# Prompt attention: a unit's value products issued behind its last transpose, and exponentials over up to 1024 columns

## The chip, the core and the metric

The kernel runs on one core of a Trainium2 chip. The metric is the device time of one launch in microseconds, the median of the timed runs. Engines are named as in the profile: PE is TensorE's matmul and PEld its weight load, DVE is VectorE, ACT is ScalarE, POOL is GpSimd, SP the engine that issues most DMAs.

## What is computed

One inference step of a decoder layer: an input projection, two kinds of heads (forgetting attention and a matrix memory), an output projection with layer norm, and an MLP with a second layer norm, for 2048 prompt tokens and for 64 sample tokens that attend to a paged cache. The change touches the forgetting attention of the prompt alone: 8 heads of 64 columns, blocks of 128 queries.

```python
def block(args):
    q_i, L_i, i = args
    s = jnp.einsum('bqhd,bkhd->bhqk', q_i, k).astype(jnp.float32) * scale
    s = s + L_i[..., :, None] - L[:, :, None, :]
    q_pos = i * Q_BLOCK + jnp.arange(Q_BLOCK)
    s = jnp.where(k_pos[None, :] <= q_pos[:, None], s, -jnp.inf)
    p = jax.nn.softmax(s, axis=-1)
    return jnp.einsum('bhqk,bkhd->bqhd', p.astype(v.dtype), v)
```

L is the running sum of the logarithms of the forget gates. The term L_i is the same along a row and drops out of the softmax, so the kernel adds only the negative sum of the keys (tile `nl`).

## The kernel before

The kernel has stages: the projections (with the matrix memory beside them), prompt attention (`phase_b`), the output projection (`phase_o`) and the MLP (`phase_c`). The sample tokens' attention to the cache is spread over the others by a pacer (`tick`), which counts up microseconds and now and then lets the next step in. In `phase_b` its pace is infinite, so that `tick` lets nothing in there.

A tile framework places the instructions: it takes them in the order in which the Python code writes them, with dependencies found from the tiles, and a scheduler that models times sets each engine's order at build. Each engine then runs its queue in that order. A tile of a pool with `bufs=n` has n places; whoever takes one waits until an earlier holder's last reader is done. `tc.issue_after(x)` adds no wait, only an order: instructions in the block come behind x on x's engine.

`phase_b` does 64 units, 8 heads times 8 pairs of query blocks. Unit g of a head has the query blocks qt = 2g and 2g+1, and query block qt has n = 128 (qt + 1) keys.

- `scores` (one unit ahead of `values`): for each query block, and for each 512 keys, two matmuls into a PSUM bank `pS` (lines 970 and 971; queries are split into a high part `qh` and a rest `ql`), from three banks in turn. VectorE adds `nl`, writes the score tile `S` and keeps the maximum in `mx` (lines 977 and 981, the latter for the diagonal block, whose mask `nd` GpSimd makes on line 963). `S` is 128 x 512, ten places.
- `values`: ScalarE takes the exponential of each `S` tile in place, with the row's sum into `lp` (line 998), and VectorE adds the sums (line 999). TensorE transposes the weights in blocks of 128 x 128, up to four into one PSUM bank `pt` (line 1011, three banks); ScalarE or VectorE copies a bank to `PT` (lines 1014 and 1016; `PT` holds four key blocks by 256 queries, four places). Then the value products (line 1020): for key block k a matmul with `vn` as weights into `po`, even k in the upper half of the array's columns and odd k in the lower. In the code, the products of four key blocks stand behind those blocks' transposes; ahead of the next four. At the end ScalarE copies the upper half and VectorE adds the lower (lines 1026 and 1028), and every fourth unit `finish` divides by the sums and stores.

A value product reads four-byte operands and leaves two records in the trace; the built program holds it as one.

Of the kernel before, what the change touches and what calls it, by code (L numbers as in the profile page):

```python
# [52 lines left out]
def body(ctx, tc, I, O, stages):  # L53
# [836 lines left out]
    def phase_b():  # L890
# [61 lines left out]
        def scores(z, g):  # L952
# [4 lines left out]
            for i in range(2):  # L957
# [8 lines left out]
                for a in range(0, n, 512):  # L966
                    b = min(n, a + 512)
                    w = max(b - a, 256)
                    pS = bank()
                    T.matmul(pS[:, :w], qh[:, qs], ks[:, a:a + w], start=True, stop=False)  # L970
                    last["PE"] = T.matmul(pS[:, :w], ql[:, qs], ks[:, a:a + w], start=False, stop=True)
                    tick(0.42)
                    sp = pb.tile([128, 512], F32, name="S", bufs=10)
                    st.append(sp)
                    e = min(b, qt * 128)
                    if e > a:
                        last["DVE"] = V.tensor_tensor_reduce(out=sp[:, :e - a], in0=pS[:, :e - a], in1=nl[:, a:e], scale=1.0, scalar=NEG,
                                               op0=OP.add, op1=OP.max, accum_out=mx[:, j:j + 1])
                        j += 1
                    if b == n:  # L980
                        V.tensor_tensor_reduce(out=sp[:, e - a:b - a], in0=pS[:, e - a:b - a], in1=nd, scale=1.0, scalar=NEG,
                                               op0=OP.add, op1=OP.max, accum_out=mx[:, j:j + 1])
                        j += 1
# [4 lines left out]
        def values(z, g, sc):  # L988
# [3 lines left out]
            for i, (st, mx) in enumerate(sc):  # L992
                qt = 2 * g + i
                n = (qt + 1) * 128
                lp = pb.tile([128, 4], F32, name="lp", bufs=6)
                for k, sp in enumerate(st):
                    w = min(512, n - k * 512)
                    last["ACT"] = A.activation(sp[:, :w], sp[:, :w], AF.Exp, bias=mx[:, 7:8], accum_out=lp[:, k:k + 1])  # L998
                V.tensor_reduce(z["ls"][:, qt:qt + 1], lp[:, :len(st)], axis=AX.X, op=OP.add)

            po = ppb.tile([128, 256], F32, name="po", bufs=1)
            nk = 2 * g + 2
            for k0 in range(0, nk, 4):
                PT = pb.tile([128, 4, 256], F32, name="PT", bufs=4)
                for i in range(2):
                    kk = min(4, 2 * g + i + 1 - k0)
                    if kk <= 0:
                        continue
                    pt = ppb.tile([128, 4, 128], F32, name="pt", bufs=3)
                    for k in range(kk):  # L1010
                        T.transpose(pt[:, k], sc[i][0][k0 // 4][:, k * 128:(k + 1) * 128], ident)
                    dst = PT[:, :kk, i * 128:i * 128 + 128]
                    if i == 0 or (k0 // 4) % 2 != 0:
                        A.copy(dst, pt[:, :kk])
                    else:
                        V.tensor_copy(dst, pt[:, :kk])
                for k in range(k0, min(k0 + 4, nk)):
                    q0 = 128 if k == nk - 1 else 0
                    c = (k % 2) * 64
                    last["PE"] = T.matmul(po[c:c + 64, q0:], z["vn"][:, k], PT[:, k - k0, q0:],  # L1020
                                          start=(k < 2), stop=(k >= nk - 2), skip_group_check=True)
                tick(0.45 * min(4, nk - k0))
            if g % 4 == 0:
                z["ot"] = pb.tile([64, 1024], F32, name="ot", bufs=2)
            od = z["ot"][:, (g % 4) * 256:(g % 4) * 256 + 256]
# [912 lines left out]
```

## Time and profile before

| | us |
|---|---|
| median of 3 timed runs | 3253.03 (3247.86 to 3255.45) |
| profiled execution | 3243.8 |
| its span, first to last instruction | 3241.8 |
| prompt attention, first score matmul to last value product | 879.1 to 1318.7, 439.6 |
| of it: 640 records of score matmuls, 1088 transposes, 1152 records of value products | |

The profile is of one execution. A row of the timeline has the start, the length, the engine, the line, the tiles (out <- in), the shape, and a count where like instructions are merged; in brackets stands the idle time before it and who ended it. A row of a window has the stretch, its length, and for PE, PEld, DVE, ACT and POOL the busy time with the number of instructions, then the clock that was granted to TensorE (1.00 is full), the DMA engines' share and GB/s. Matmuls overlap, so that the distance from one start to the next, not the length, is what one costs TensorE.

### The profile page before, as it was taken

To read this page: it belongs to the slowest core of one execution; us is meant where nothing else is said; L and a number is where in the kernel's file an instruction comes from. 1 tells how busy PE (TensorE), PEld (TensorE's weight loads), DVE (VectorE), ACT (ScalarE), POOL (GpSimd) and SP (SyncE) were. 2 spreads that over 40 slices of the span, in tenths; PEclk is the share of its full clock that TensorE was granted. 3 is DMA by queue.
4 is the path that set the end of the run, shared out by engine and by line. 5 is a ranking of instruction groups with operands and counts; after the bars stand their busy time and mean duration, and the time that the engine had idled before them with its cause. 6 is when DMAs were issued, how large, how long until landed. Compare 5 with 4: busy or idle time off the path is not lost.

```text
span 3241.8 us, 58017 instructions
## 1 busy us (share of the span) xinstructions
PE 3132.6 (97%) x21681; PEld 2552.5 (79%) x21681; DVE 2105.9 (65%) x5083; ACT 1502.6 (46%) x2965; POOL 916.0 (28%) x974
## 2 busy tenths in 40 slices
PE   8999999999899999999999999999999999899997
PEld 8898999999866667677677777677777777788895
DVE  6856557465488887543556568565686666866658
ACT  4343344334388888412444445343453444544442
POOL 0121324333333333475333324333334121000000
PEclk9999999999999999999999999999999999999998
DMA  5565866777676865686787869778879566543332
GB/s 189 147 214 168 263 216 243 255 244 264 195 257 169 203 177 126 223 297 243 291 297 268 305 241 335 296 265 313 295 282 342 201 231 215 188 164 119 116 105 100
DMA packets 339777, 734.36 MB, mean 227 GB/s; under 512 B 63656, under 2 KB 177704, under 8 KB 338600
## 3 DMA queue, kind: packets, MB, share of 16 engines
q1 hardware_dynamic: 252360, 416.18, 39.7%
q0 software_dynamic: 83520, 304.12, 26.6%
q10 hardware_dynamic: 3616, 10.36, 0.9%
q8 instruction: 171, 2.80, 0.3%
q14 instruction: 110, 0.90, 0.1%
HBM read 677.71 MB, written 86.38 MB: 236 GB/s over the span
## 4 chain that ended last, share of the span: by engine, by line
PE 44%; DMA 4%; DVE 3%; issue 1%; POOL 0%; ACT 0%; DVEq 0%; ACTq 0%; POOLq 0%
PE ph L163 8%; PE ph L164 7%; PE ph L165 7%; PE py L163 6%; PE py L165 5%; PE py L164 5%; PE sO L1790 3%; DMA vt<-cache_v,idxV 2%; PE sQ L1678 2%; DMA xr<-cache_v,idxV 1%; DVE y L1351 1%; DVE wl L157 1%; PE sT L1747 1%; DMA kT<-cache_k,idxK 0%; POOL vt L1766 0%
## 5 line engine op out<-in xcount | busy, mean ns | idle before, releaser
L157 DVE TENSOR_TENSOR wl<-wr,wh 128x1024 fp32r<-128x1024 f32 x364 | 444.2, 1222 | 376.3 <-ACT wh L154 374.9
L154 ACT ACTIVATE wh<-wr 128x1024 fp32r<-128x1024 f32 x364 | 383.0, 1054 | 331.2 <-PE ph L164 175.7
L163 PE MATMUL ph<-x1h,wh 128*128 128x512 f32 (+1 forms) x1280 | 455.0, 355 | 1.1 <-ACT hq L1333 1.1
L164 PE MATMUL ph<-x1l,wh 128*128 128x512 f32 (+1 forms) x1280 | 452.5, 354 | 0.2 <-DVE x1l L157 0.2
L165 PE MATMUL ph<-x1h,wl 128*128 128x512 f32 (+1 forms) x1280 | 450.1, 353 | 0.0
L1655 POOL DMA_INDIRECT kT<-cache_k,idxK x256 | 275.6, 1077 | 536.3 <-PE sQ L1678 470.5
L163 PE MATMUL py<-wh,hh 128*128 128x512 f32 x896 | 357.3, 401 | 3.0 <-ACT hh L154 1.5
L164 PE MATMUL py<-wl,hh 128*128 128x512 f32 x896 | 352.5, 393 | 3.4 <-DVE wl L157 3.4
L165 PE MATMUL py<-wh,hl 128*128 128x512 f32 x896 | 350.0, 394 | 2.0 <-DVE hl L157 2.0
L1351 DVE TENSOR_TENSOR y<-y,py 128x512 f32<-128x512 f32 x416 | 280.6, 681 | 64.0 <-PE py L165 59.3
L163 PE MATMUL pm<-xh,whi 128*128 128x256 f32 (+1 forms) x1024 | 298.9, 292 | 0.0
L164 PE MATMUL pm<-xl,whi 128*128 128x256 f32 (+1 forms) x1024 | 294.8, 288 | 0.0
L165 PE MATMUL pm<-xh,wlo 128*128 128x256 f32 (+1 forms) x1024 | 293.8, 287 | 0.0
L1766 POOL DMA_INDIRECT vt<-cache_v,idxV x164 | 180.3, 1100 | 384.4 <-PE sO L1790 315.3
L163 PEld LDWEIGHTS ph<-x1h,wh 128*128 128x128 f32 x1280 | 240.4, 188 | 42.0 <-issue 7.8
L164 PEld LDWEIGHTS ph<-x1l,wh 128*128 128x128 f32 x1280 | 240.5, 188 | 33.8 <-issue 3.3
L165 PEld LDWEIGHTS ph<-x1h,wl 128*128 128x128 f32 x1280 | 240.1, 188 | 34.1 <-issue 3.7
L163 PE MATMUL pm<-whi,xh 128*128 128x256 f32 (+2 forms) x816 | 236.9, 291 | 9.2 <-ACT whi L154 8.2
L164 PE MATMUL pm<-wlo,xh 128*128 128x256 f32 (+2 forms) x816 | 232.5, 285 | 0.6 <-DVE wlo L157 0.6
L165 PE MATMUL pm<-whi,xl 128*128 128x256 f32 (+2 forms) x816 | 232.2, 285 | 0.0
L998 ACT ACTIVATE S<-S,mx 128x512 f32<-128x512 f32 (+2 forms) x320 | 207.8, 653 | 19.0 <-DVE mx L984 17.6
L163 PEld LDWEIGHTS py<-wh,hh 128*128 128x128 f32 x896 | 168.6, 189 | 51.4 <-issue 10.9
(372 smaller groups left out, 6799.7 us busy)
## 6 DMA issues: line engine op xcount, KB each, us to landing
wr<-w SPq DMA_DIRECT2D x224, 512.0 KB
wr<-dw SPq DMA_DIRECT2D x128, 512.0 KB
wra<-w_in SPq DMA_DIRECT2D x104, 512.0 KB
dw<-w POOLq DMA_DIRECT2D x48, 512.0 KB, 8.4
Rb<-dR SPq DMA_DIRECT2D x128, 128.0 KB
xn<-xp_t SPq DMA_DIRECT2D x16, 512.0 KB
qn<-dq SPq DMA_DIRECT2D x128, 64.0 KB
kn<-k_prompt SPq DMA_DIRECT2D x64, 128.0 KB
```

Source lines behind the costliest of these rows:

```text
L154: last["ACT"] = A.activation(dst, src, AF.Copy, scale=scale)
L157: r = (eng or V).tensor_tensor(dst, src, hi.bitcast(F32), op=OP.subtract)
L163: T.matmul(ps, wh, xh, start=first, stop=False, skip_group_check=shared)
L164: T.matmul(ps, wh, xl, start=False, stop=False, skip_group_check=shared)
L165: last["PE"] = T.matmul(ps, wl, xh, start=False, stop=stop, skip_group_check=shared)
L998: last["ACT"] = A.activation(sp[:, :w], sp[:, :w], AF.Exp, bias=mx[:, 7:8], accum_out=lp[:, k:k + 1])
L1351: V.tensor_tensor(y, y, ps, op=op)
L1655: G.indirect_dma_start(out=piece(n), out_offset=None, in_=ck, in_offset=IO(ap=idxK[:, b, j // 2, j % 2:j % 2 + 1], axis=0))
L1678: r = T.matmul(pq[h4 * 32:h4 * 32 + 32, hg].rearrange("p (k c) -> p k c", k=2), z["qb"][:, hd], kv, start=(db == 0), stop=(db == 1), skip_ ...
L1747: T.transpose(p[:, f], z["U"][u][:, hg, f].rearrange("p k t -> p (k t)"), ident)
L1766: vx["last"] = G.indirect_dma_start(out=vt.rearrange("p f c -> p (f c)"), out_offset=None, in_=cv, in_offset=IO(ap=idxV[:, b, (kt % 4) * 4 ...
L1790: after_ = T.matmul(po[r:r + 32], z["PT"][:, hg, 2 * f + g, pg].rearrange("p h q -> p (h q)"), vts[f][:, g, hg * 256:(hg + 1) * 256], star ...
```

## The change

Two things change in `phase_b`. A score tile now has 1024 columns (seven places for ten), VectorE fills it in two steps of 512 as before, and one exponential covers up to 1024 columns; `lp` keeps two sums in place of four. And `values` writes all transposes and copies of a unit first, keeps its list of `PT` tiles, and then all its value products, each ordered behind the unit's last transpose (`turned`). The `tick` in `values` goes. `PT` keeps its four places, which is what the longest unit (16 key blocks) uses.

```diff
-                    sp = pb.tile([128, 512], F32, name="S", bufs=10)
-                    st.append(sp)
+                    if a % 1024 == 0:
+                        st.append(pb.tile([128, 1024], F32, name="S", bufs=7))
+                    sp = st[-1][:, a % 1024:a % 1024 + 512]
...
-                lp = pb.tile([128, 4], F32, name="lp", bufs=6)
+                lp = pb.tile([128, 2], F32, name="lp", bufs=6)
                 for k, sp in enumerate(st):
-                    w = min(512, n - k * 512)
+                    w = min(1024, n - k * 1024)
                     last["ACT"] = A.activation(sp[:, :w], sp[:, :w], AF.Exp, bias=mx[:, 7:8], accum_out=lp[:, k:k + 1])
...
+            PTs = []
             for k0 in range(0, nk, 4):
                 PT = pb.tile([128, 4, 256], F32, name="PT", bufs=4)
+                PTs.append(PT)
...
                     for k in range(kk):
-                        T.transpose(pt[:, k], sc[i][0][k0 // 4][:, k * 128:(k + 1) * 128], ident)
+                        c = k0 % 8 * 128 + k * 128
+                        turned = T.transpose(pt[:, k], sc[i][0][k0 // 8][:, c:c + 128], ident)
...
-                for k in range(k0, min(k0 + 4, nk)):
-                    q0 = 128 if k == nk - 1 else 0
-                    c = (k % 2) * 64
-                    last["PE"] = T.matmul(po[c:c + 64, q0:], z["vn"][:, k], PT[:, k - k0, q0:],
+            for k in range(nk):
+                q0 = 128 if k == nk - 1 else 0
+                c = (k % 2) * 64
+                with tc.issue_after(turned.ins):
+                    last["PE"] = T.matmul(po[c:c + 64, q0:], z["vn"][:, k], PTs[k // 4][:, k % 4, q0:],
                                           start=(k < 2), stop=(k >= nk - 2), skip_group_check=True)
-                tick(0.45 * min(4, nk - k0))
```

The scheduler then sets another order. TensorE's queue, in the longest unit of the fifth head (16 key blocks), before; the unit's own products read `po_15285`, its last transposes fill `pt_15338` and `pt_15343`, and the transposes into `pt_15407` and `pt_15410` and the scores belong to later units:

```order
L1011 MATMUL pt_15327<-ident_74,S_15150 128x128 x4
L1020 MATMUL po_15285<-PT_15286,vn_13898 64x256 x4
L970 MATMUL pS_15485<-ks_14708,qh_15452 128x512
...
L1020 MATMUL po_15285<-PT_15303,vn_13898 64x256 x4
L1011 MATMUL pt_15338<-ident_74,S_15130 128x128 x3
...
L1011 MATMUL pt_15343<-ident_74,S_15155 128x128 x4
L1020 MATMUL po_15285<-PT_15320,vn_13898 64x256 x4
L1011 MATMUL pt_15407<-ident_74,S_15253 128x128
L970 MATMUL pS_15500<-ks_14708,qh_15452 128x512
...
L1011 MATMUL pt_15410<-ident_74,S_15262 128x128 x2
...
L1020 MATMUL po_15285<-PT_15337,vn_13898 64x256 x3
L1020 MATMUL po_15285<-PT_15337,vn_13898 64x128
```

Where rows are left out there are only score matmuls: two stand between the first runs of products, two ahead of `pt_15343`, four ahead of `pt_15410` and four ahead of the last run. The products come in four runs. The same unit in the changed program, where each left-out row is the second score matmul of a pair:

```order
L1015 MATMUL pt_15166<-ident_74,S_14976 128x128 x3
L1015 MATMUL pt_15171<-ident_74,S_14999 128x128 x4
L1025 MATMUL po_15125<-PT_15126,vn_13798 64x256 x4
L1025 MATMUL po_15125<-PT_15139,vn_13798 64x256 x4
L1025 MATMUL po_15125<-PT_15152,vn_13798 64x256 x4
L1015 MATMUL pt_15247<-ident_74,S_15097 128x128
L970 MATMUL pS_15328<-ks_14576,qh_15290 128x384
...
L1015 MATMUL pt_15250<-ident_74,S_15106 128x128 x2
L970 MATMUL pS_15337<-ks_14576,qh_15290 128x512
...
L1025 MATMUL po_15125<-PT_15165,vn_13798 64x256 x3
L1025 MATMUL po_15125<-PT_15165,vn_13798 64x128
```

Four runs of products have become two: twelve products stand together behind the last transposes, and the last four follow behind three transposes and four score matmuls.

ScalarE's queue near the end of the stage, before; the exponentials are those of the last two query blocks (n = 1920 and 2048), the copies those of the last two units:

```order
L998 ACTIVATE S,lp<-S,mx 128x512 x3
L998 ACTIVATE S,lp<-S,mx 128x384
L1014 COPY PT<-pt 128x4x128 x3
L1014 COPY PT<-pt 128x128
L1014 COPY PT<-pt 128x2x128
L998 ACTIVATE S,lp<-S,mx 128x512 x4
L1014 COPY PT<-pt 128x4x128
```

And in the changed program:

```order
L999 ACTIVATE S,lp<-S,mx 128x1024
L999 ACTIVATE S,lp<-S,mx 128x896
L1018 COPY PT<-pt 128x4x128
L1018 COPY PT<-pt 128x128
L999 ACTIVATE S,lp<-S,mx 128x1024 x2
L1018 COPY PT<-pt 128x2x128
L1018 COPY PT<-pt 128x4x128
```

Eight exponentials have become four over the same columns, and the last block's stand ahead of two copies that they stood behind. Ahead of this stage the engines' orders are the same; behind it, TensorE's, VectorE's, ScalarE's and SP's differ in a few places by neighbours that change places, and GpSimd's not at all.

## The prediction

> **What bounds the kernel now.** I read the engines' totals first, to see which engine the time is made of, and then cut the span into stretches (busy time of each engine, granted clock and DMA share), to see the attention stage by itself.
>
> ```profile
> PE 3132.6 (97%) x21681; PEld 2552.5 (79%) x21681; DVE 2105.9 (65%) x5083; ACT 1502.6 (46%) x2965; POOL 916.0 (28%) x974
> ...
> 879.10:904.00 24.90, 18.41 (x92) 12.64 (x93) 15.70 (x69) 15.03 (x45) 4.71 (x11) 0.73 0.75 206
> 904.00:1308.00 404.00, 395.46 (x2712) 274.76 (x2710) 327.60 (x1296) 341.49 (x961) 145.33 (x225) 1.00 0.68 180
> 1308.00:1318.70 10.70, 10.07 (x82) 6.51 (x78) 3.21 (x10) 6.59 (x17) 0.26 (x1) 1.00 0.08 25
> ```
>
> Over the whole span TensorE is the bound, and prompt attention is the 439.6 us from 879.1 to 1318.7. In its long middle, TensorE is busy for 395.46 of 404.00 us, so it idles for 8.5 us; ScalarE is at 85% (341.49) and VectorE at 81% (327.60). The change removes no TensorE work, so it can gain in two ways only: TensorE's idle time, and what a change from one kind of matmul to another costs. The next view, waits on TensorE in that middle stretch (total, times, longest), says who ends the idle time.
>
> ```profile
> PE pt L1011 <- ACT S L998: 1.4, 3, 0.5
> PE pt L1011 <- ACT PT L1014: 1.2, 1, 1.2
> PE pS L970 <- DVE mx L977: 1.2, 1, 1.2
> PE pS L970 <- DVE ls L999: 1.0, 1, 1.0
> PE pS L970 <- DVE mx L981: 0.8, 2, 0.6
> PE po L1020 <- DVE ot L1028: 0.7, 1, 0.7
> PE pS L970 <- DVE mx L984: 0.4, 2, 0.2
> PE pt L1011 <- DVE PT L1016: 0.4, 2, 0.2
> PE pt L1011 <- DVE lt L1038: 0.2, 1, 0.2
> PE po L1020 <- ACT PT L1014: 0.2, 1, 0.2
> ```
>
> These add up to 7.5 us: 2.8 behind ScalarE (exponentials and copies of the transposed tiles) and 4.7 behind VectorE. They are few and short; no single place repeats at a price that matters.
>
> **The change: TensorE's order.** What does a change of kind cost? The timeline of TensorE from 1296 us on holds every kind (start, length, line, tiles, count; each value product leaves two records, so x16 is eight products).
>
> ```profile
> 1296.13 0.49 PE L1011 MATMUL pt<-ident,S 128*128 128x128 f32 x3
> 1296.37 0.47 PE L970 MATMUL pS<-ks,qh 128*128 128x512 f32 x1
> 1296.69 0.39 PE L971 MATMUL pS<-ks,ql 128*128 128x512 f32 x1
> 1296.92 1.03 PE L1011 MATMUL pt<-ident,S 128*128 128x128 f32 x8
> 1297.71 0.48 PE L970 MATMUL pS<-ks,qh 128*128 128x512 f32 x1
> 1298.03 0.40 PE L971 MATMUL pS<-ks,ql 128*128 128x512 f32 x1
> 1298.35 1.95 PE L1020 MATMUL po<-PT,vn 128*64 128x256 f32 x16
> 1300.23 0.44 PE L970 MATMUL pS<-ks,qh 128*128 128x384 f32 x1
> 1300.51 0.34 PE L971 MATMUL pS<-ks,ql 128*128 128x384 f32 x1
> 1300.69 0.60 PE L1011 MATMUL pt<-ident,S 128*128 128x128 f32 x4
> 1301.22 1.08 PE L1020 MATMUL po<-PT,vn 128*64 128x256 f32 x8
> 1302.23 0.50 PE L970 MATMUL pS<-ks,qh 128*128 128x512 f32 x1
> 1302.56 0.39 PE L971 MATMUL pS<-ks,ql 128*128 128x512 f32 x1
> 1302.79 0.39 PE L970 MATMUL pS<-ks,qh 128*128 128x512 f32 x1
> ```
>
> Read the starts, not the lengths, since matmuls overlap. Eight products take 1298.35 to 1300.23, 1.88 us; four take 1301.22 to 1302.23, 1.01 us. So a product is 0.2175 us, and a run of them pays 1.01 - 4 x 0.2175 = 0.14 us once. It also pays on entry: the score matmul ahead of it holds TensorE for 0.32 us (1298.03 to 1298.35), where one ahead of another score or a transpose holds it for 0.23 (1296.69 to 1296.92, 1302.56 to 1302.79): 0.09 us. A run of value products thus costs 0.23 us by being a run. Going between scores and transposes costs nothing: eight transposes ahead of a score take 0.79 us (0.11 each and 0.02 for the last), which gives back what the first score matmul pays behind them (0.32 for 0.23). Behind value products nothing is given back: the first score matmul there pays 0.33 (1302.23 to 1302.56), 0.10 too much.
>
> In the built order I counted 116 runs of value products before and 98 now, nearly all of the fewer in the two longest units of a head. Scores stand directly behind such a run 36 times before and 53 times now. That is -18 x 0.23 + 17 x 0.10 = -4.1 + 1.7, **about -2.4 us**. Ahead of the last products of a long unit now stand the twelve earlier ones (12 x 0.2175 = 2.6 us) with a few scores and transposes. The copies of the last transposes, which they need, lie beside that; were the cover gone, a copy (0.56 us, last row of the next fence) would stand open in each of 64 units, 36 us, so the order of the rows decides. In the unit shown in the section on the change, there lie between last transpose and last products twelve products, three transposes and four score matmuls now, 2.75 + 0.15 + 1.2 = 4.1 us, and four products, three transposes and eight score matmuls before, 1.0 + 0.15 + 2.1 = 3.3. No new wait is expected there.
>
> **The change: exponentials.** ScalarE's own timeline prices one exponential with its sum.
>
> ```profile
> 1297.80 0.71 ACT L998 ACTIVATE S<-S,mx 128x512 f32<-128x512 f32 x1
> 1298.42 0.19 ACT L998 ACTIVATION_READ_ACCUMULATOR S<-S,mx 128x1 f32 x1
> 1298.51 0.71 ACT L998 ACTIVATE S<-S,mx 128x512 f32<-128x512 f32 x1
> 1299.12 0.19 ACT L998 ACTIVATION_READ_ACCUMULATOR S<-S,mx 128x1 f32 x1
> 1299.22 0.49 ACT L998 ACTIVATE S<-S,mx 128x256 f32<-128x256 f32 x1
> 1299.62 0.19 ACT L998 ACTIVATION_READ_ACCUMULATOR S<-S,mx 128x1 f32 x1
> 1299.71 0.56 ACT L1014 COPY PT<-pt 128x512 f32<-128x512 f32 x1
> ```
>
> 512 columns hold ScalarE for 0.71 us (1297.80 to 1298.51) and 256 for 0.49 (1299.22 to 1299.71). So 256 columns are 0.22, and 0.27 us is fixed. A head has 40 exponentials before and 24 now, 320 and 192 in all; the columns stay. ScalarE loses 128 x 0.27 = 35 us of work, some 32 of them in the middle stretch: 341 falls to about 309 us, 85% to 77%. None of this is on TensorE's path by itself. It counts only where a transpose or a product waits for ScalarE: the 2.8 us above. The Trainium skill ("Perfetto Trace Analysis", Optimizing Scalar/DVE Operations) gives about 93 ns of overhead for each ScalarE instruction on SBUF; by that estimate two instructions for each of 128 exponentials would be 24 us less work, and the sum for TensorE would be the same.
>
> A row of scores now lies in tiles of 1024 columns, seven of them, in place of ten of 512. A unit with two rows of 2048 columns filled eight of ten, and two blocks of the next unit could start; now it fills four of seven, and three of the next unit's four can. The wait that this loosens stands on VectorE:
>
> ```profile
> DVE S L977 <- PE pt L1011: 19.8, 31, 1.8
> ```
>
> VectorE waited 31 times for a transpose to give a score tile free, and while it waits, the score matmuls behind it find their PSUM bank full. That is one source of TensorE's waits for VectorE. How much of them goes, no row says: the bounds are nothing and 4.7 us, and I take half, 2.3. The 2.8 us behind ScalarE I take as gone, being short and ScalarE being 32 us lighter: **about -5.1 us** in all, between 0 and -8.5.
>
> **What costs nothing.** The removed tick only feeds a pacer whose pace is infinite in this stage. The two partial sums fewer in a row of lp leave the VectorE reduction one instruction, as it is. The small first units (879 to 904, 6.5 us idle) begin in the same order. In the later stages the order moves a few VectorE, ScalarE and SP rows; on SP two cache-bias loads go ahead of the load of a third token tile. I bound that by the largest single wait above, 1.2 us, to either side, and take 0.
>
> The sum is -2.4 - 5.1 = -7.5 us. The profiled execution took 3243.8 us, its span 3241.8; it would become 3236.3. That execution lies 9.2 below the median of the timed runs, 3253.0, and below all of them (3247.9 to 3255.5), so I carry over the difference: **3245.5 us**.
>
> **Rivals.** *The waits stay.* TensorE idles for 8.5 us in a stage of 404, and each wait may be made by the new order itself. Then only the runs gain: 3253.0 - 2.4 = 3250.6. For it speaks that 4.7 of the 7.5 us end at VectorE, which gets no less to do. Chance 0.27.
>
> *All of the idle time goes* as well, and with it 1.5 us of the first units: -2.4 - 8.5 - 1.5 = -12.4, 3240.6. Chance 0.15.
>
> *The coarse exponential is late.* A transpose of a row of 1024 columns or more now starts behind an exponential of 0.27 + 4 x 0.22 = 1.15 us, 0.44 more than before. There are nine such rows in a head, 72 in all. If ScalarE delivered just in time everywhere, this would be 72 x 0.44 = 32 us. Against it: TensorE waited for an exponential 3 times in 404 us, so the rows are mostly done well ahead. It decides from the point at which ScalarE's lead is under 0.44 us in a third of the rows: 24 x 0.44 = +10.6, less 2.4, +8 us, 3261. The same page and section of the Trainium skill says that where Scalar isn't saturated but causes bubbles on other engines, breaking up instructions may let work finish sooner; by that rule this change goes the wrong way, and the 1.4 us of bubbles behind exponentials is what the trace has of it so far. Chance 0.15.
>
> *The clock drops.* Runs of eleven transposes or more become 16 from 11. What a drop costs is seen at the start of the next stage (interval of matmuls of 512 columns):
>
> ```profile
> 1324.05 0.63 PE L163 MATMUL pw<-wh,mh 128*128 128x512 f32 x1
> 1324.47 0.63 PE L164 MATMUL pw<-wl,mh 128*128 128x512 f32 x1
> ...
> 1327.20 0.40 PE L165 MATMUL pw<-wh,ml 128*128 128x512 f32 x1
> 1327.44 0.40 PE L163 MATMUL pw<-wh,mh 128*128 128x512 f32 x1
> ```
>
> 0.42 us there against 0.24 later; over 3.4 us that is about 1.5 us lost. Five more such drops are +7.5, and with the forecast's -7.5 the time is 3253. The Trainium skill ("TensorE: Matmul & The Clock Gate", Part 4) says that the full clock doesn't engage for transposes, which don't count as TensorE being busy in the same way; by it these runs would be dangerous. The granted clock of 1.00 from 904 to 1318.7, with 11 such runs in the stage, speaks against it. Chance 0.03.
>
> **How the numbers follow.** My forecast (-4 to -11 us) has 0.40, the waits that stay 0.27, the larger gain 0.15, the late exponential 0.15, the clock 0.03. A measurement of this kernel tells about 0.2%, 6.5 us, from no change: faster means under 3246.5, slower over 3259.5. The forecast is split by that line, six tenths of it beyond: 0.24 + 0.15 + some of the first rival's spread (the timed runs differ by 7.6 us), 0.44. Slower has the late exponential and a little of the second spread, 0.18; the rest, 0.38, is within. The range goes from the larger gain less a spread of 4, 3236, to the late exponential, 3261.
>
> **What would show it.** Right: 192 exponentials of line 999, ScalarE at some 77% between the same units, fewer than 8.5 us of TensorE idle time in the middle, VectorE's wait for transposes well under 19.8 us, and the stage's end about 7 us sooner with the later stages unmoved. Wrong: rows in which TensorE waits for S behind line 999 more than a few times; ScalarE's copies waiting for value products, which would mean that a unit's four transposed tiles are held too long; or a stage as long as before at a lighter ScalarE, which would mean that the waits came from the order and not from the load. A lower clock between 904 and 1308 would be the last rival.

## The result, and the profile after

The change takes 3244.52 us (3230.43 to 3255.17 in 19 runs) where the kernel before takes 3252.51 (3244.84 to 3263.79 in 19): a ratio of 0.9975, 95% interval 0.9965 to 0.9985, or 8.0 us less. The forecast was 3245.5, 7.5 less. The runs go with the granted clock: the eight of the change below 3240 us have 0.988 to 0.990, the eleven above 3244 have 0.986 to 0.988. The number is right; whether the reasons are is another question, and the profile of the change (of its run of 3251.05 us) raises it at once. First the page's totals of the change, then its attention stage in stretches (busy time of PE, PEld, DVE, ACT and POOL, then clock, DMA share and GB/s).

```profile
PE 3134.1 (96%) x21681; PEld 2562.6 (79%) x21681; DVE 2108.0 (65%) x5083; ACT 1466.9 (45%) x2709; POOL 910.8 (28%) x974
```

```profile
889.90:904.00 14.10, 8.22 (x26) 5.29 (x26) 7.10 (x32) 4.67 (x13) 3.14 (x8) 0.56 0.77 210
904.00:1320.00 416.00, 401.64 (x2764) 286.21 (x2763) 342.52 (x1336) 316.29 (x740) 147.05 (x229) 0.99 0.67 180
1320.00:1331.10 11.10, 11.06 (x93) 7.34 (x91) 2.52 (x6) 6.50 (x14) 1.26 (x1) 1.00 0.07 25
```

ScalarE has 256 instructions fewer (2709 for 2965), which are the 128 exponentials with their sums, and stands at 316.29 of 416.00 us, 76%: as forecast. But the stage is not shorter. It runs from 889.9 to 1331.1, 441.2 us, against 439.6 before, and TensorE's idle time in the long middle (904 to 1320 here, 904 to 1308 before) is 416.00 - 401.64 = 14.4 us, against 8.5. The waits in that middle say what came and what went (waiting engine and line, what ended it, total, times, longest).

```profile
ACT ks L154 <- DMA kn<-k_prompt: 8.0, 4, 4.8
ACT ks L154 <- DMA drl<-lt: 4.0, 2, 3.3
PE pt L1015 <- ACT PT L1018: 6.3, 3, 3.6
PE pS L970 <- DVE mx L978: 3.4, 2, 1.7
DVE S L978 <- PE pt L1015: 2.1, 4, 0.8
PE pt L1015 <- ACT S L999: 0.4, 1, 0.4
```

VectorE's wait for a score tile, which was 19.8 us in 31 places, is 2.1 in 4, and TensorE's wait for an exponential is 0.4 us in place of 1.4. Those two went as the prediction had it. In their place stands a wait that it does not name: TensorE waits 6.3 us in three places for ScalarE's copies, and ScalarE has waited 8.0 us in four places for a load of keys. (The profile puts two more waits of that split, the longer one of 3.31 us, to a store, `drl<-lt`; the split reads no `drl`, and in the second profile of the change the same wait, 3.61 us, stands under the load of keys.) The longest of them, first on ScalarE, then on TensorE, then SP's issues of the load, which comes in two halves:

```profile
1114.50 0.59 ACT L1018 COPY PT<-pt 128x512 f32<-128x512 f32 x1
1119.91 0.63 ACT L154 ACTIVATE ks<-kn 128x512 fp32r<-128x512 f32 x1 [4.81 <-DMA kn<-k_prompt]
1120.45 1.05 ACT L1018 COPY PT<-pt 128x512 f32<-128x512 f32 x2
```

```profile
1117.12 0.40 PE L971 MATMUL pS<-ks,ql 128*128 128x512 f32 x1
1121.07 1.75 PE L1015 MATMUL pt<-ident,S 128*128 128x128 f32 x7 [3.55 <-ACT PT L1018]
```

```profile
1110.57 1.25 SPq L925 DMA_DIRECT2D kn<-k_prompt  x2
```

Each head splits four tiles of keys for the next head, and `kn` has three places. So the fourth load is issued only when a place is free: here at 1110.57 and 1111.15, right behind the last reader of the first tile (VectorE's half of the split, 1109.31 to 1110.34), and the split starts 8.8 us after the second half's issue. ScalarE takes its queue in order: the split that needs the load holds up the copies behind it, and the transposes wait for those. The load is as slow in the kernel before (issued 1099.71, split 9.25 us later). But there the fourth split stands 17 ScalarE rows behind the third, in the change 12 or 13, so less of the load is covered. The longest wait before stands first here; VectorE's half of the split waits with it, and TensorE waits for VectorE:

```profile
1108.96 0.63 ACT L154 ACTIVATE ks<-kn 128x512 fp32r<-128x512 f32 x1 [3.51 <-DMA kn<-k_prompt]
1109.62 0.69 DVE L157 TENSOR_TENSOR ks<-kn,ks 64x512 fp32r<-64x512 f32 x1 [2.28 <-ACT ks L154]
1111.46 0.47 PE L970 MATMUL pS<-ks,qh 128*128 128x512 f32 x1 [1.02 <-DVE ls L999]
```

Two profiles of each kernel, cut at the first matmul, the first score matmul, the last value product, the end of the output projection and the last instruction, in us (the span also has some 8 us ahead of the first matmul):

| profile | projections | attention | output projection | MLP | span |
|---|---|---|---|---|---|
| before | 870.9 | 439.5 | 229.1 | 1694.0 | 3241.8 |
| before, again | 879.5 | 444.3 | 223.9 | 1693.2 | 3249.3 |
| change | 881.8 | 441.1 | 221.6 | 1696.5 | 3249.1 |
| change, again | 874.7 | 441.1 | 224.3 | 1691.0 | 3238.8 |

The projections differ by 11 us among profiles although nothing in them was changed, so the span of a single profile cannot show 8 us. What can be compared is the stage, and there the change has gained 0.8 us against the mean of the two profiles of before. By head (from the end of one head's last value product to that of the next), the second takes 51.5 us in the change and 53.4 before, in both profiles of each. The third and fourth take 56.3 and 57.1 (57.0 and 57.5 in the second profile) against 52.6 and 54.6 (52.6 and 56.3). These two are the heads with the late keys; the fourth is long in the second profile of the kernel before as well. The last two heads are alike in both kernels: 50.7 and 46.8 us against 50.9 and 46.8.

### The profile page after: what moved, and what is told of

Same layout as the page of the kernel before. It is cut to its first block, busy times and chain, and to the rows that moved or that the text cites. A ratio compares the mean times of both kernels' runs of the same rounds, so it can differ in the third digit from the quotient of the medians.

```text
span 3249.1 us, 57784 instructions
## 1 busy us (share of the span) xinstructions
PE 3134.1 (96%) x21681; PEld 2562.6 (79%) x21681; DVE 2108.0 (65%) x5083; ACT 1466.9 (45%) x2709; POOL 910.8 (28%) x974
## 4 chain that ended last, share of the span: by engine, by line
PE 44%; DMA 4%; DVE 2%; issue 1%; POOL 0%; ACT 0%; DVEq 0%; ACTq 0%; POOLq 0%
PE ph L163 8%; PE ph L164 7%; PE ph L165 7%; PE py L163 6%; PE py L165 5%; PE py L164 5%; PE sO L1794 2%; DMA vt<-cache_v,idxV 2%; PE sQ L1682 2%; DMA xr<-cache_v,idxV 1%; DMA kT<-cache_k,idxK 1%; DVE y L1355 1%; PE sT L1751 1%; DVE wl L157 1%; DVE y L192 0%
## 5 line engine op out<-in xcount | busy, mean ns | idle before, releaser
L157 DVE TENSOR_TENSOR wlo<-wra,whi 128x1024 fp32r<-128x1024 f32 (+1 forms) x112 | 141.7, 1268 | 105.4 <-ACT whi L154 105.0
```

The lines of the kernel that those rows point to most:

```text
L157: r = (eng or V).tensor_tensor(dst, src, hi.bitcast(F32), op=OP.subtract)
```

## The experiments

### Repeats, and each half alone

The kernel before and the change were run again unaltered, beside two kernels that have one half of the change each. The first half is the wide tiles and exponentials; the value products stay where they were (shown against the change):

```diff
-                        turned = T.transpose(pt[:, k], sc[i][0][k0 // 8][:, c:c + 128], ident)
+                        T.transpose(pt[:, k], sc[i][0][k0 // 8][:, c:c + 128], ident)
...
-            for k in range(nk):
-                q0 = 128 if k == nk - 1 else 0
-                c = (k % 2) * 64
-                with tc.issue_after(turned.ins):
-                    last["PE"] = T.matmul(po[c:c + 64, q0:], z["vn"][:, k], PTs[k // 4][:, k % 4, q0:],
+                for k in range(k0, min(k0 + 4, nk)):
+                    q0 = 128 if k == nk - 1 else 0
+                    c = (k % 2) * 64
+                    last["PE"] = T.matmul(po[c:c + 64, q0:], z["vn"][:, k], PT[:, k - k0, q0:],
```

The second half (shown against the kernel before) is the products behind the last transpose, with score tiles and exponentials of 512 columns:

```diff
-                        T.transpose(pt[:, k], sc[i][0][k0 // 4][:, k * 128:(k + 1) * 128], ident)
+                        turned = T.transpose(pt[:, k], sc[i][0][k0 // 4][:, k * 128:(k + 1) * 128], ident)
...
-                for k in range(k0, min(k0 + 4, nk)):
-                    q0 = 128 if k == nk - 1 else 0
-                    c = (k % 2) * 64
-                    last["PE"] = T.matmul(po[c:c + 64, q0:], z["vn"][:, k], PT[:, k - k0, q0:],
+            for k in range(nk):
+                q0 = 128 if k == nk - 1 else 0
+                c = (k % 2) * 64
+                with tc.issue_after(turned.ins):
+                    last["PE"] = T.matmul(po[c:c + 64, q0:], z["vn"][:, k], PTs[k // 4][:, k % 4, q0:],
```

The change again: 

> The changed kernel once more, to see what is chance in its profile. Theory A (TensorE's stage gets shorter, but the fourth key load of a head, with three places for key tiles, now comes late on ScalarE and gives part back): a ratio of 0.996 to 0.999; the attention stage between 428 and 442 us, longer by about as much as the ScalarE waits for key tiles (6 to 12 us in all) put on TensorE, and 12 us shorter where those waits are absent. Rival B (the gain is not in the attention stage, which was 441.1 us in the changed profile and 439.5 before): the stage is 439 to 442 us again, whatever the key loads do.

The kernel before again: 

> The kernel before, against itself. Both theories: a ratio of 1.000 within 0.002, a stage of 437 to 441 us. A: at most one or two waits of ScalarE for the fourth key tile of a head, since it stands 17 or 18 rows behind the third there and 13 in the changed program. The projections ahead of the stage took 10.8 us longer in the changed profile with the same order; if that is chance, this run's lie anywhere between 870 and 882.

Wide tiles alone: 

> Score tiles and exponentials of 1024 columns, value products where they were before. 120 runs of products (116 before) and scores behind a run 46 times (36): by prices, TensorE pays 4 x 0.23 + 10 x 0.10 = 1.9 us more. ScalarE is 35 us lighter as in the change. A: waits shrink but the fourth key tile comes early on ScalarE (12 to 15 rows behind the third) as in the change: ratio 0.997 to 1.001. If the lighter ScalarE is what gains, this has most of the change's gain, 0.998; if the order is, it has none, 1.000 or more.

Moved products alone: 

> Value products behind the unit's last transpose, score tiles and exponentials of 512 columns as before. 101 runs of products, scores behind a run 34 times: by prices -15 x 0.23 - 2 x 0.10 = -3.7 us. ScalarE as loaded as before; the fourth key tile 14 rows behind the third. A: -3.7 us less what the key loads take, 0.998 to 1.001. If the order is what gains, 0.9975 as the whole change; if it is the lighter ScalarE, 0.999.

| kernel | us | ratio to before, 95% interval |
|---|---|---|
| change, again | 3240.82 | 0.9961 [0.9947, 0.9975] |
| before, again | 3253.22 | 1.0007 [0.9994, 1.0019] |
| wide tiles alone | 3245.81 | 0.9988 [0.9973, 1.0004] |
| moved products alone | 3250.67 | 1.0002 [0.9988, 1.0016] |

The gain of the change is there again. Neither half alone can be told from no change by its time; the interval of the wide tiles reaches from -0.27% to +0.04%. At this size the times leave open which half does it. The profiles point one way: the stage is 436.6 us with the wide tiles alone and 446.6 with the moved products alone, against 439.5 and 444.3 before and twice 441.1 in the change. Late keys are in both: with the wide tiles alone ScalarE waits 5.63 us and TensorE 4.27 behind it in the fourth head, with the moved products alone 2.84 and 2.41.

### A fourth place for the keys

If the late key load gives back part of the gain, a fourth place for `kn` returns it. The room comes from two small tiles of `finish`; the same edit was made to the change and to the kernel before.

```diff
-            kn = pb.tile([128, 512], F32, name="kn", bufs=3)
+            kn = pb.tile([128, 512], F32, name="kn", bufs=4)
...
-            lr = pb.tile([128, 32], F32, name="lr", bufs=2)
+            lr = pb.tile([128, 32], F32, name="lr", bufs=1)
...
-            lt = pb.tile([128, 32], F32, name="lt", bufs=2)
+            lt = pb.tile([128, 32], F32, name="lt", bufs=1)
```

In the change: 

> The change, with four places for the key tiles kn in place of three (paid for by one place in place of two for the two small tiles of finish). All four of a head's key splits then stand together on ScalarE; with three places the fourth waits there for its load (4.81 and 3.31 us in the profile of the change), and TensorE stood still behind it (3.55 and 2.44 us) and came back at half clock. Theory: the late key load gives back a good part of what the change wins; without it no ScalarE wait for a key tile over 1 us, an attention stage of 428 to 434 us in place of 441, ratio 0.993 to 0.996 to the kernel before. Rival: the key loads cost nothing that another wait doesn't take over, stage 440 to 442 us, ratio 0.996 to 0.998 as for the change.

In the kernel before: 

> The kernel before, with the same four places for the key tiles. ScalarE waited 3.51 us at most for a key tile there, and TensorE 1.2 us at most for ScalarE. Theory: the late load costs the kernel before little, since its splits stand 17 rows apart: ratio 0.999 to 1.001, stage 438 to 442 us. Rival: the places for keys are worth the same to both kernels, ratio 0.996 to 0.998, as much below the kernel before as the change with four places is below the change.

The change with four places takes 3241.86 us, ratio 0.9961 [0.9949, 0.9973]; the kernel before with four places 3255.32, ratio 1.0014 [1.0003, 1.0025]. In the profile the theory has its way. The stage is 433.9 us, third and fourth head 50.7 and 53.2, and from 904 us on ScalarE waits for keys only in the first head (the two waits are at 911.7 and 916.9):

```profile
ACT ks L154 <- DMA kn<-k_prompt: 3.8, 2, 2.6
```

By time it does not: 0.9961 is also what the unaltered change had in the batch before. The 7 us that the profile shows are not in the medians, so the theory in that form, that the late load costs the change several microseconds of its timed runs, is not borne out. The kernel before is a little slower with the four places; its profile (of one of its longest runs, 3263.36 us) has no late key either, but a stage of 450.9 us, with 8.0 us of TensorE's waits behind VectorE's copies (the scheduler put other rows there as well).

### The stage three times as long

At 8 heads an effect of 0.2% is as large as the spread. So the stage was given 24 heads in place of 8: the eight heads are computed three times, with the same values, and the rest of the program stays (`h % 8` likewise where keys and queries are loaded and the output is stored).

```diff
-            h = z["h"]
+            h = z["h"] % 8
...
-        units = [(h, g) for h in range(8) for g in range(8)]
+        units = [(h, g) for h in range(24) for g in range(8)]
```

From the tenth head to the twenty-first the heads repeat one pattern, and the DMA share, 0.67 in the 8-head stage, is 0.31 to 0.32. Five kernels were run in this form: before, the change, each half, and the change with exponentials of 512 columns over its wide score tiles:

```diff
-                lp = pb.tile([128, 2], F32, name="lp", bufs=6)
-                for k, sp in enumerate(st):
-                    w = min(1024, n - k * 1024)
+                lp = pb.tile([128, 4], F32, name="lp", bufs=6)
+                for k in range((n + 511) // 512):
+                    sp = st[k // 2][:, k % 2 * 512:k % 2 * 512 + 512]
+                    w = min(512, n - k * 512)
...
-                V.tensor_reduce(z["ls"][:, qt:qt + 1], lp[:, :len(st)], axis=AX.X, op=OP.add)
+                V.tensor_reduce(z["ls"][:, qt:qt + 1], lp[:, :(n + 511) // 512], axis=AX.X, op=OP.add)
```

The kernel before: 

> The kernel before with the attention stage over 24 heads in place of 8: the eight heads are computed three times, with the same values. It is there to be compared with the next one. 16 more heads of about 53.4 us (the steady heads of the trace of before): 3252 + 854 = 4106 us.

The change: 

> The change with the attention stage over 24 heads. TensorE has 290 runs of value products in place of 348 and 165 score matmuls behind one in place of 100: -58 x 0.23 + 65 x 0.10 = -6.8 us. Theory that the change gains in the stage, head by head: three times the 8 us of the change, 20 to 28 us below the 24 heads of the kernel before. Theory that only the runs count: 7 us below. Rival, that the gain lies in the stages behind the attention or in how they start, since the stage of the profiled change is no shorter than before: 0 to 10 us below.

Wide tiles alone: 

> 24 heads, score tiles and exponentials of 1024 columns, value products where they stood before. TensorE's order has 332 runs of value products (348 in the 24 heads of the kernel before, 290 in those of the change) and 143 score matmuls behind one (100, 165), so runs give -16 x 0.23 + 43 x 0.10 = +0.6 us. Theory that waits and runs add up and that the wider tiles take the waits: the steady head falls from 52.74 us to 52.0 to 52.2, the whole by 12 to 17 us, to 4078 to 4083. Rival, that the waits go only with the products moved too: steady head 52.6 to 52.9, time 4090 to 4098.

Moved products alone: 

> 24 heads, value products behind the unit's last transpose, score tiles and exponentials of 512 columns as before. 309 runs of value products and 98 score matmuls behind one: -39 x 0.23 - 2 x 0.10 = -9.2 us, 0.38 a head. Theory that waits and runs add up and the order takes the runs only: steady head 52.2 to 52.5 us, time 4083 to 4090. Rival, that the order takes the waits too and the wider tiles do nothing: steady head as in the change, 51.3 to 51.6, time 4074 to 4082. Third, that moving the products makes waits of its own with the heavier ScalarE: steady head 52.6 or more.

The change with short exponentials: 

> 24 heads of the change (score tiles of 1024 columns in seven places, value products behind the last transpose) with exponentials of 512 columns, so that ScalarE keeps the 128 instructions for every eight heads that the change takes away: 59.4 us of work in a steady head in place of 52.0. 274 runs of value products and 127 score matmuls behind one. Theory that the lighter ScalarE takes the waits: they come back, steady head 52.0 us or more, time 4083 to 4095. Rival, that the room for score tiles and the order take them: steady head 51.0 to 51.5, time 4070 to 4080, at most as long as the change.

Now the twelve steady heads of each, as one stretch, in this order: before, moved products alone, the change with short exponentials, wide tiles alone, the change.

```profile
1400.80:2033.60 632.80, 626.31 (x4322) 435.96 (x4321) 518.95 (x2065) 545.42 (x1537) 162.12 (x252) 1.00 0.31 91
```

```profile
1395.60:2043.60 648.00, 626.47 (x4321) 439.66 (x4321) 510.15 (x2067) 545.99 (x1536) 152.25 (x252) 1.00 0.31 89
```

```profile
1386.10:2008.90 622.80, 613.92 (x4321) 442.35 (x4320) 515.08 (x2065) 539.00 (x1538) 166.59 (x252) 1.00 0.32 92
```

```profile
1385.90:2002.30 616.40, 616.08 (x4322) 438.50 (x4321) 519.28 (x2065) 495.56 (x1155) 158.31 (x253) 1.00 0.32 94
```

```profile
1386.70:2003.30 616.60, 613.60 (x4321) 439.00 (x4321) 514.25 (x2065) 490.12 (x1153) 161.29 (x252) 1.00 0.32 94
```

The first two numbers are the length and TensorE's busy time; TensorE is at full clock in all five. Read with the timed medians, and with two sums worked out from the starts of successive matmuls in these twelve heads: the number of runs of value products, and how much the intervals exceed the median of their kind, where they do by more than 0.04 us ("late"). A kind is a matmul's shape with what stands ahead of it and behind it, and the median is over all five kernels. The first and the last row of the table were measured together, the other three together at another time, when the kernel before had a median of 3250.01 us in place of 3253.50; so the ratio to the 8-head kernel before, measured beside each, is the better comparison across the two.

| kernel, 24 heads | us | ratio, 95% interval | one steady head, us | runs a head | scores behind a run, a head | late, 12 heads, us |
|---|---|---|---|---|---|---|
| before | 4095.11 | 1.2586 [1.2565, 1.2608] | 52.74 | 14.5 | 4 | 16.8 |
| moved products alone | 4118.51 | 1.2664 [1.2639, 1.2690] | 54.00 | 13 | 4 | 37.7 |
| change, short exponentials | 4084.96 | 1.2566 [1.2541, 1.2591] | 51.90 | 11.5 | 5.5 | 17.8 |
| wide tiles alone | 4071.35 | 1.2522 [1.2498, 1.2547] | 51.37 | 13 | 6 | 5.7 |
| change | 4077.84 | 1.2531 [1.2505, 1.2557] | 51.39 | 12 | 7 | 8.4 |

**The gain lies in the stage.** The change is 17.3 us below the kernel before, twice what it gains at 8 heads, and 1.35 us in every steady head. Three times 8 would have been 24; 20 to 28 were expected, so this was missed by some 3 us, and with five runs of each the times alone would also allow the rival's 10. What decides is the profile: its stage is 26.9 us shorter (1262.5 for 1289.4), and the MLP of the two profiles differs the other way by 8.8.

**The wide tiles carry it alone.** They gain 23.8 us (20.8 by the ratios), more than the theory's 12 to 17 and far from the rival's waits that go only with the products moved. Their steady head, 51.37, is that of the whole change. TensorE is idle for 616.40 - 616.08 = 0.3 us in twelve heads. This holds for the order that the scheduler made for 24 heads: there the wide tiles also have fewer runs of value products, 13 a head for 14.5, where in the 8-head kernel they had four more, 120 for 116.

**Moving the products without them makes the stage slower**, by 23.4 us (25.4 by the ratios) and 1.26 a head; the theory that the order gives its runs and nothing else (4083 to 4090) falls, and the third guess, waits of its own, holds, though the rows put them behind VectorE and not ScalarE. These are TensorE's waits in the twelve heads, with VectorE's for a score tile, of moved products alone:

```profile
PE pS L971 <- DVE mx L978: 12.4, 12, 1.1
PE pt L1014 <- DVE PT L1019: 7.9, 24, 0.5
DVE S L978 <- PE pt L1014: 34.0, 60, 1.8
```

Before:

```profile
PE pt L1012 <- DVE PT L1017: 2.1, 8, 0.5
PE pt L1012 <- ACT S L999: 1.9, 4, 0.5
PE pS L971 <- DVE mx L985: 1.1, 6, 0.2
DVE S L978 <- PE pt L1012: 31.0, 49, 1.8
```

The change:

```profile
PE pS L971 <- DVE mx L983: 2.7, 11, 0.3
PE pS L971 <- DVE ls L1001: 0.3, 1, 0.3
ACT ks L154 <- DMA kn<-k_prompt: 5.6, 8, 1.0
ACT PT L1019 <- PE po L1026: 6.8, 12, 0.6
```

And the change with short exponentials:

```profile
PE pS L971 <- DVE mx L983: 5.2, 12, 0.4
PE pt L1017 <- DVE mx L986: 3.3, 6, 0.6
DVE S L979 <- PE pt L1017: 5.1, 12, 0.6
```

With ten tiles of 512, VectorE waits 31 to 34 us for a transpose to free a score tile, and TensorE waits behind VectorE; with seven of 1024 that wait is gone (no row for it in the change), 7.2 us with the wide tiles alone, or 5.1 with the short exponentials. Since it is nearly the same before and with the products moved, it does not say by itself why the late time more than doubles there. The lighter ScalarE is the other part: put the short exponentials back and the late time goes from 8.4 to 17.8 us, TensorE's idle time from 3.0 to 8.9, the head from 51.39 to 51.90. That was expected as 52.0 or more if the lighter ScalarE took the waits and 51.5 at most if it did not, so the first is nearer; the time, 4084.96, lies in the first one's range, though its interval and the change's overlap. Both parts matter, the room for scores most where the products have been moved (54.00 to 51.90). Short exponentials over wide tiles with the products left in place were not run.

### Where the late keys come from

From 933 to 1278 us of the change's profile GpSimd issues 64 transfers that build sums of w2 for the MLP, about ten a head. The first 16 store; the next 16 accumulate, and these fall beside the third and fourth head (those after them, which read the sums themselves, begin at 1113). One kernel leaves all 32 accumulating ones out, so part of w2's combinations is missing.

```diff
+        if more:
+            return
         with tc.issue_after(last["POOL"].ins):
```

> The change (8 heads) with the 32 accumulating ones of the 64 sums of w2 left out, whose transfers run beside heads 1 to 5 and hold the DMA engines at some 0.7 to 0.8 of the time there; without any the share was 0.32 in the steady heads of the 24. Part of w2's combinations is therefore missing from the output. Theory that these transfers make the key tiles late and so the third and fourth head long (56.3 and 57.1 us): no ScalarE wait over 1.5 us for a key tile behind the first head, those heads at 51 to 53 us, stage 427 to 433 us in place of 441, time 6 to 14 us below the change. Rival, that the order of these heads makes the waits: the two heads stay at 55 to 57 us, the time within 3 us of the change.

It takes 3233.53 us, ratio 0.9944 [0.9924, 0.9964]: 11.0 us below the change's first median and 7.3 below its second, in the range that the theory gave; by the ratios, since these runs were not taken side by side, 10 and 5.5 us, and the interval overlaps that of the second. The stage is 429.4 us. The stretch of the second to fourth head, first in the change, then here:

```profile
964.00:1123.00 159.00, 152.08 (x1043) 108.77 (x1043) 130.40 (x499) 119.98 (x281) 60.10 (x93) 0.98 0.75 198
```

```profile
964.00:1123.00 159.00, 157.30 (x1102) 112.14 (x1101) 133.85 (x529) 124.88 (x294) 52.94 (x84) 1.00 0.51 153
```

The DMA share falls from 0.75 to 0.51 and TensorE's idle time from 6.9 to 1.7 us. ScalarE's waits for keys become shorter, and TensorE no longer feels them, though they don't vanish as expected:

```profile
ACT ks L154 <- DMA kn<-k_prompt: 9.3, 9, 2.1
```

The third and fourth head take 52.7 and 52.1 us, within the 51 to 53 expected. The fourth load of the fourth head now lands 5.2 us after the issue of its second half, where it took 8.7 in the change and 9.2 in the kernel before; where ScalarE waits for one in the steady heads of the 24, it is 3.6 to 4.9. So the transfers are what makes the late load long enough to reach TensorE. Whether the kernel before would gain as much without them was not tried, so it is not shown that the change suffers more from them than the kernel before in timed runs.

## Why the prediction was right, and where it was not

**Right by its total: -7.5 forecast, -8.0 measured** (-10.8 in the repeat, by 3251.63 for the runs of before in that batch). That it fits to half a microsecond is luck: the runs of the two kernels spread over 19 and 25 us, and the 8-head profile does not show the gain where the prediction put it. What the forecast rests on has to be judged on the steady heads of the 24, where neither the first head nor the late keys disturb.

*The runs, -2.4 us: the mechanism held, and the size was too small.* The prices were seen again: a score matmul of 512 columns ahead of a value product holds TensorE for 0.326 us and ahead of another score for 0.233, a transpose for 0.202 and 0.109, and a score behind products for 0.337 in place of 0.233. But the prediction priced what stands behind a run only where it is a score. A transpose directly behind a run takes 0.166 us ahead of another transpose, in place of 0.109: 0.057 too much. With it, -30 runs x 0.23 + 36 scores x 0.104 - 66 transposes behind a run x 0.057 (126 before, 60 now) = -6.9 + 3.7 - 3.8 = -7.0 us in twelve heads, -4.7 in eight. The transposes are 2.5 of that. (In the built order of the 8 heads the transposes behind a run go from 79 to 44, and the sum is -4.4.)

*The waits, -5.1 us: about the right size.* The late time falls from 16.8 to 8.4 us in twelve heads, -5.6 in eight. Together with the runs that is -15.4 us of the 16.2 by which twelve heads became shorter. The same sum, with 84, 108 and 72 transposes behind a run, gives -15.1 for the wide tiles alone (measured -16.4), +15.7 for the moved products alone (+15.2) and -8.5 for the short exponentials (-10.0). So the prices of the runs and the late time account for all four within some 1.5 us. The prediction looked for this in TensorE's idle time, and there only 3.5 of it stands (6.5 to 3.0): most of a wait lies inside the modelled length of the matmul before, and the page counts it as busy. The prediction could have found more of it in the intervals between starts. That the size fits is partly luck too. Of the 7.5 us of waits that it read, 1.2 behind ScalarE's copies and 1.0 behind VectorE's sums stood right behind a split that waited for its load of keys (1.62 us at 915.26, and the 3.51 shown above). A lighter ScalarE does not shorten those, and in the 8-head profile the idle time that should have fallen rose by 5.9 us.

*Its reason for the waits held; its attribution to the two halves did not.* It laid the runs to the moved products and the waits to the wide tiles. In the steady heads the wide tiles alone take both: 13 runs a head and 5.7 us of late time. Moving the products on top takes one more run a head, adds a score behind a run, and adds 2.7 us of late time in twelve heads, so that it is worth nothing there. The step that failed is "No new wait is expected there". Of the products themselves it is true: in the steady heads no row has one that waits for a copy. But alone, the moved products make 20.9 us more of late time in twelve heads, ahead of scores and transposes, and what covers them in the change is the room for score tiles and the lighter ScalarE. The prediction treated the two edits as a sum, and they are not one.

*What it did not foresee* is the key load. Nothing in the prediction names `ks<-kn`; its waits of up to 3.5 us on ScalarE were in the trace of before, where TensorE stood still for about 1 us behind the longest (1.1 in the second profile). With the third and fourth split closer together TensorE waited twice, for 2.44 and 3.55 us, and each pause had 3.4 us of half clock at its end. That is 2.44 + 3.55 + 2 x 1.7 = 9.4 us in the profile of the change. Six steady heads, since the last two are alike, give 6 x 1.35 = 8.1, so it accounts for a profiled stage that is no shorter. Why the timed runs gain all the same stays open. The fourth place took this wait away and the median did not move: either the wait costs less in most of the timed runs, or the four places cost as much elsewhere. The second pair of profiles belongs to runs near their medians, 3240.78 and 3251.40 us; of the 10.5 us between their spans the stage has 3.2 and the projections, whose order is the same, 4.8.

*The signs named:* ScalarE's share and VectorE's wait came as forecast. TensorE's idle time and the stage's end did not, for the reason above. A stage as long as before at a lighter ScalarE was named as a sign of being wrong, and it came. It was to mean that the waits come from the order; here it is the order of the key splits on ScalarE, of which the prediction did not think. ScalarE's copies do wait for value products (6.8 us in twelve heads), which was named as a sign against; TensorE has no wait behind them, so it does no harm. It is not the moved products' doing either: before it is 2.6 us, with the wide tiles alone 8.8.

*The rivals.* The late exponential would have shown as TensorE waiting for S; there is one such wait of 0.4 us in the long middle of the stage and none in twelve steady heads. An exponential of 1024 columns took 1.15 us as estimated, and ScalarE lost 55 us in twelve heads, 4.6 each, where 16 x 0.27 = 4.3 was forecast. The rule of the Trainium skill ("Perfetto Trace Analysis", Optimizing Scalar/DVE Operations) that breaking up instructions may let work finish sooner is not borne out here: with the exponentials broken up the head became 0.5 us longer. The clock: the granted clock is 1.00 over all twelve heads, with one run of eleven transposes and seven of eight in each. Eleven transposes last 1.2 us, and no longer run is in these heads. The rule of the Trainium skill ("TensorE: Matmul & The Clock Gate", Part 4), that the full clock does not engage for transposes, is not seen here.

No kernel was found that is surely faster than the change. Wide tiles alone, and the change with four key places, cannot be told from it: 3245.81 and 3241.86 us against 3244.52 and 3240.82, and 4071.35 against 4077.84 for the wide tiles alone with 24 heads.

## What to carry to other kernels

Two edits that each look good on TensorE's order need not add up: run each alone, and where the effect is no larger than the spread of the runs, repeat the changed stage several times over and read the steady part. Count waits by the distances between starts of like matmuls, since idle time by the page of the profile held only 3.5 of the 8.4 us that went. And when an in-order engine gets lighter or its rows move, look for the load that one of its rows needs: with one place fewer than there are loads, the last one's issue depends on the order of that very engine.

## What the runs showed of the hardware

All fourteen pauses of TensorE of 2.1 us or more in the attention stages of the fourteen profiles (leaving out each stage's first 24 us) have a stretch of half clock at their end. It begins between 2.7 us ahead of the pause's end and 2.0 behind it. It lasts 3.4 us for the eleven pauses of up to 3.6 us and 6.8 for the three of 4.3 to 4.6. Of thirteen pauses of 1.5 to 1.9 us two have one, and one stretch of half clock has no pause over 1.2 us ahead of it. Here is the longest pause in the first profile of the change. Granted clock is the third column from the end; the stretches are ahead of the pause, the pause, and what follows.

```profile
1110.00:1117.50 7.50, 7.25 (x49) 4.82 (x47) 6.67 (x28) 5.10 (x14) 2.49 (x6) 1.00 1.02 250
1117.50:1120.80 3.30, 0.01 (x1) 0.00 (x0) 0.23 (x1) 0.89 (x2) 0.00 (x0) 1.00 0.80 309
1120.80:1124.20 3.40, 3.13 (x15) 2.23 (x17) 3.34 (x15) 3.38 (x9) 0.58 (x2) 0.50 0.43 141
1124.20:1130.00 5.80, 5.80 (x45) 3.80 (x42) 2.83 (x14) 2.69 (x7) 3.05 (x5) 1.00 0.58 150
```

So this pause of 3.5 us costs about 5.2, by estimate: half of 3.4 on top. And leaving the value products has a price by what follows: 0.10 us with a score matmul, 0.057 with a transpose.
